# Gathering the experts of 64 tokens, running the other 192 through full products, and starting a transformer kernel in quarters

## The chip, the core and the metric

The kernel runs on one core of a Trainium2 chip. The core has five engines with instruction streams of their own: TensorE (PE in the profile, with its weight loads as PEld), VectorE (DVE), ScalarE (ACT), GpSimd (POOL) and SyncE (SP, which here only issues DMAs). All data comes from HBM through 16 DMA engines. The metric is the device time of one execution in microseconds (us); lower is better.

## The reference, cut to what matters

A two-layer transformer block over 256 tokens with 256 context tokens, then a second block with a convolution and recurrence mixer and a layer of experts (PEER), then a last normalization. The two places that the change touches:

```python
m_lat = silu(c) @ ada_w[i] + ada_b[i]          # 6 x 1024 modulation values; the same with c_ctx
sh1, sc1, g1, sh2, sc2, g2 = split(m_lat, 6)
h  = rms(x, norm1_g[i]) * (1.0 + sc1) + sh1    # hc likewise for the context
f, q, k, v = split(h @ w_in)                   # first projections
...
def peer(x, wq, keys, u_tab, v_tab):           # 256 tokens, 16384 experts
    q = (x @ wq).reshape(B, L, 8, 2, 128)      # 8 heads
    s = einsum('blhpd,hpkd->blhpk', q, keys)
    ts, ti = top_k(s, 16)
    cs, ci = top_k(all pairs of the two halves, 16)
    experts = e1 * 128 + e2                    # 8 * 16 = 128 experts for each token
    act = gelu(einsum('td,tkd->tk', x, u_tab[experts])) * softmax(cs)
    return einsum('tk,tkd->td', act, v_tab[experts])
```

`u_tab` and `v_tab` have 16384 rows of 1024 float32 numbers each (67 MB each).

## The kernel before

**Products.** A float32 product runs as three products in the type fp32r: each operand is split into a high part (a copy by ACT) and a low part (a subtraction by DVE; `split`, L326 and L327), and `mm3` (L331 to L333) multiplies high by high, low by high and high by low into one accumulator in PSUM. A matmul has a stationary operand, loaded as weights (128x128 at most), and a moving one that streams past it, one column after the other; its tile is printed as 128*128 with the moving shape behind it.

**The slab stream.** All weights come as slabs of 128x1024 float32 (512 KB). `Stream.get` keeps loads two slabs ahead: SP issues the DMA into `raw`, ACT makes `hi`, DVE makes `lo`, and a slab of a projection then takes 24 matmuls (8 pieces of the contraction, three products). `crit` is an instruction behind which slab loads are held.

**The start.** Silu of the two conditions is spread over all partitions (`cbc`). The modulations of layer 0 and 1 come from tiles of 128x1024 of the modulation weights, most of them in an idle moment of DVE: one multiply and reduce over 1024 columns (L450) for each of two conditions. The first five tiles (NAK) go to PE instead: `ada_first` (L436) has 128 weight columns stationary and two moving columns. The first 16 tiles must be there before the first norm is applied: 5 by PE, 11 by DVE (22 instructions). Meanwhile `x_sums`, `sums_add` and `sums_done` square x and the context (ACT), add up (POOL, L475), and take the inverse root (POOL, L366). `norm_mod` applies norm and modulation to all 8 pieces of 128 channels, and only then do the slabs of the first projections start, in the order key, value, four queries.

**PEER.** 16 slabs of `peer_wq` and the scores; then a dense computation. All 16384 experts are computed for all 256 tokens, and those that a token did not choose get the gate 0.
- `inner(j, tn)`: slab j of u, stationary, against the 256 tokens as moving columns; gelu into `big[:, j, :]` (128 slabs x 256 tokens). The first J1 = 56 slabs run before and under `select` (the two top-k, on DVE), which lays out expert numbers and gates in `eT`.
- The gates stage: `gates4` takes four tokens at a time. DVE and ACT build one-hot tables (B L1353, A L1363), PE multiplies them (L1365) into the gates of all 16384 experts, DVE multiplies `big` by them. 64 such groups alternate with the other 72 slabs of u.
- The v stage: for each of 128 slabs of v, `big[:, j, :]` is split (`ah`, `al`), and the tokens are stationary (two halves of 128), the slab moving in two halves of 512 columns: 12 matmuls. The four accumulators are [tokens, channels].
- The tail: residual and last norm on DVE and ACT (L1500 the last multiply), four output DMAs.

Tiles are scheduled by a list scheduler at compile time; each engine runs its instructions in order.

## Time and profile before

| what | us |
|---|---|
| median of 3 runs | 2120.29 |
| range of the runs | 2119.91 to 2121.41 |
| the profiled execution | 2122.77 |
| its span, from the first to the last instruction | 2120.9 |

The profiled execution is one execution of the program under the hardware profiler. Its span is 1.9 us shorter than its own time. In a window's row each engine's busy time stands with its number of instructions; a busy PE may still be pausing inside its matmuls, because they are pipelined. [...]

### The profile page before, as it was taken

What the parts mean: (1) busy time and instruction counts of PE and PEld (TensorE: products, weight loads), DVE (VectorE), ACT (ScalarE), POOL (GpSimd) and SP (SyncE); (2) the same over time, 40 slices, a digit from 0 to 9 for tenths busy, and PEclk for the clock granted to TensorE, in tenths of its full rate; (3) what the DMA queues carried; (4) which work ended last, traced back from release to release, by engine and by line L of the source; (5) the groups of instructions that cost most, each with busy time, mean ns of one, the idle gap of its engine ahead of it and who ended that gap; (6) DMA issues with size and microseconds to landing.
All of it is one profiled execution on the core that took longest, in us unless ns stands there. A gap on an engine that the chain in (4) does not pass through costs nothing.

```text
span 2120.9 us, 34014 instructions
## 1 busy us (share of the span) xinstructions
PE 2054.7 (97%) x12714; PEld 1803.1 (85%) x12714; DVE 1511.1 (71%) x2853; ACT 1086.4 (51%) x1997; POOL 150.4 (7%) x194
## 2 busy tenths in 40 slices
PE   6999899999999999999999999999999999999998
PEld 4857677888878857999898999999999998888886
DVE  7795999674756485555578877996677886666666
ACT  3366332332335464444586844555677765454544
POOL 4001100000010001000124311000000000000000
PEclk9989899999999999999999999999999999999999
DMA  8242457796843324555776465556544446566563
GB/s 319 92 140 75 150 195 252 233 328 207 284 136 109 120 87 142 180 186 179 238 255 215 133 195 175 175 189 190 167 146 145 149 149 203 195 192 196 192 195 129
DMA packets 115649, 383.90 MB, mean 181 GB/s; under 512 B 12611, under 2 KB 21092, under 8 KB 115228
## 3 DMA queue, kind: packets, MB, share of 16 engines
q1 hardware_dynamic: 106146, 358.32, 51.6%
q0 software_dynamic: 4048, 15.47, 2.0%
q10 hardware_dynamic: 5290, 7.94, 1.2%
q8 instruction: 100, 1.64, 0.3%
q14 instruction: 65, 0.53, 0.1%
HBM read 366.08 MB, written 15.60 MB: 180 GB/s over the span
## 4 chain that ended last, share of the span: by engine, by line
PE 87%; DVE 5%; ACT 3%; issue 2%; POOL 1%; DMA 1%; SPq 0%; ACTq 0%; DVEq 0%; POOLq 0%
PE pa L331 26%; PE pa L333 25%; PE pa L332 25%; PE pb L1365 3%; PE pb L620 2%; DVE adaj L450 1%; PE pb L607 1%; PE pa L707 1%; DVE lo L327 1%; PE pb L984 1%; PE pa L866 1%; ACT hi L326 1%; DMA adaw<-in_ada_n 1%; POOL ix L1058 0%; PE pb L505 0%
## 5 line engine op out<-in xcount | busy, mean ns | idle before, releaser
L326 ACT ACTIVATE hi<-raw 128x1024 fp32r<-128x1024 f32 (+2 forms) x534 | 552.4, 1037 | 628.9 <-PE pa L332 430.1
L327 DVE TENSOR_TENSOR lo<-raw,hi 128x1024 fp32r<-128x1024 f32 (+2 forms) x534 | 641.6, 1204 | 281.8 <-ACT hi L326 233.4
L331 PE MATMUL pa<-nhi,hi 128*128 128x256 f32 (+1 forms) x1504 | 430.8, 287 | 5.1 <-ACT sg L1214 3.1
L333 PE MATMUL pa<-nhi,lo 128*128 128x256 f32 (+1 forms) x1504 | 425.8, 284 | 0.0
L332 PE MATMUL pa<-nlo,hi 128*128 128x256 f32 (+1 forms) x1504 | 425.7, 284 | 0.0
L331 PEld LDWEIGHTS pa<-nhi,hi 128*128 128x128 f32 x1504 | 286.0, 191 | 6.8 <-ACT sg L1214 3.5
L332 PEld LDWEIGHTS pa<-nlo,hi 128*128 128x128 f32 x1504 | 285.8, 190 | 0.0
L333 PEld LDWEIGHTS pa<-nhi,lo 128*128 128x128 f32 x1504 | 285.6, 190 | 0.0
L332 PE MATMUL pa<-lo,hi 128*128 128x512 f32 (+1 forms) x704 | 238.3, 339 | 0.0
L331 PE MATMUL pa<-hi,hi 128*128 128x512 f32 (+1 forms) x704 | 235.5, 340 | 2.8 <-ACT hi L326 2.7
L333 PE MATMUL pa<-hi,lo 128*128 128x512 f32 (+1 forms) x704 | 236.7, 339 | 0.0
L332 PE MATMUL pa<-lo,ah 128*128 128x512 f32 x512 | 198.9, 389 | 0.0
L333 PE MATMUL pa<-hi,al 128*128 128x512 f32 x512 | 198.2, 389 | 0.0
L450 DVE CUSTOM_DVE_ANT_0 adaj<-adaw,cbc,vec 128x1024 bf16<-128x1024 f32 x150 | 195.7, 1339 | 2.6 <-ACT cbc L420 1.3
L331 PEld LDWEIGHTS pa<-hi,hi 128*128 128x128 f32 x704 | 134.8, 193 | 19.0 <-ACT hi L326 3.3
L332 PEld LDWEIGHTS pa<-lo,hi 128*128 128x128 f32 x704 | 135.3, 192 | 14.7 <-DVE lo L520 0.8
L333 PEld LDWEIGHTS pa<-hi,lo 128*128 128x128 f32 x704 | 135.2, 192 | 13.8
L326 ACT ACTIVATE ah<-big 128x256 fp32r<-128x256 f32 x128 | 53.4, 418 | 168.5 <-PE pa L332 167.1
L331 PE MATMUL pa<-hi,ah 128*128 128x512 f32 x512 | 138.9, 389 | 0.0
L331 PE MATMUL pa<-fh,hi 128*128 128x512 f32 (+1 forms) x352 | 117.7, 337 | 0.5 <-ACT hi L326 0.5
L332 PE MATMUL pa<-fl,hi 128*128 128x512 f32 (+1 forms) x352 | 117.8, 336 | 0.0
L333 PE MATMUL pa<-fh,lo 128*128 128x512 f32 (+1 forms) x352 | 116.5, 336 | 0.0
(376 smaller groups left out, 3540.8 us busy)
## 6 DMA issues: line engine op xcount, KB each, us to landing
raw<-in_u SPq DMA_DIRECT2D x128, 512.0 KB, 3.5
raw<-in_v SPq DMA_DIRECT2D x128, 512.0 KB, 4.3
adaw<-in_ada_n SPq DMA_DIRECT2D x91, 512.0 KB, 4.4
raw<-in_ffn_gu SPq DMA_DIRECT2D x88, 512.0 KB, 3.5
raw<-in_w_in SPq DMA_DIRECT2D x63, 512.0 KB, 4.5
raw<-in_ffn_d SPq DMA_DIRECT2D x32, 512.0 KB, 3.5
raw<-in_od_in SPq DMA_DIRECT2D x24, 512.0 KB, 3.5
low<-lo POOLq DMA_DIRECT2D x19, 512.0 KB, 5.5
```

The source lines that it names most:

```text
L326: self.nc.scalar.activation(out=hi, in_=src, func=AF.Copy)
L327: return self.nc.vector.tensor_tensor(lo, src, hi.bitcast(F32), op=ALU.subtract)
L331: mm(ps, L[0], R[0], start=start, stop=False)
L332: mm(ps, L[0], R[1], start=False, stop=False)
L333: self.last_mm = mm(ps, L[1], R[0], start=False, stop=stop)
L450: nc.vector.tensor_tensor_reduce(j, w, self.cbc[:, s, :], 1.0, self.v(f"ada_b{l}", m), ALU.mult, ALU.add, accum_out=self.mods[l][:, m, s:s ...
L607: nc.tensor.transpose(pt[:, k, :], P[:, e, 128 * k:128 * k + 128], self.ident)
L620: self.nc.tensor.matmul(po[b, :], vt(e, k), PTs[e][:, k, :], start=k == 0, stop=k == kc - 1)
L707: nc.tensor.matmul(S[kv], qT[i][b, q0:q0 + 128], kT[b, k0:k0 + nk], start=True, stop=True)
L866: nc.tensor.matmul(S[e], qT[b, i, 128 * qt:128 * qt + 128], kT[b, i, :], start=True, stop=True)
L984: nc.tensor.matmul(ps, raw[:tn, c, tc, :], kp[c][:tn, tc, :], start=tc == 0, stop=tc == 2)
L1365: nc.tensor.matmul(ps[:, k, :], A, B[:, k, :], start=True, stop=True)
```

## The change

**The start.** NAK is 16. `ada_block(b)` computes four modulation tiles on PE with the condition stationary (32 columns, of which two are used, in one of four column strips) and 512 weight columns moving, 8 matmuls in float32; a copy by ACT and four small matmuls add the strips and turn the result. Block b gives shift and scale of channels 256 b to 256 b + 255. DVE's 22 reductions and `ada_first` go. `cbc` is made by 16 matmuls and four DVE copies. `first_sums` adds squares on DVE instead of POOL and takes the inverse root on DVE. Four slab loads are issued between block 0 and block 1; `first_products` applies norm and modulation to two channel pieces as each block is done, and multiplies them with the first four slabs (key, value, two queries).

**PEER.** The last 64 tokens (TS) no longer go through the dense computation. `sparse` takes 64 steps over u and 64 over v. On the 128 partitions stand the 64 tokens twice. Step c issues an indirect DMA from POOL that gathers one row of u into each partition (512 KB): of each token's 128 experts, number c into its first and number 64 + c into its second partition. DVE multiplies them with x and reduces (128x1024); gelu and gate follow once for all. A step over v gathers likewise, and DVE multiplies and adds (128x1024) into `acc`, whose two halves are added at the end by a matmul for each 512 channels. Five buffers (NROW) take the gathered rows. Of the 129 steps 46 stand in the gates stage, one in each group from the third on, and 83 under the first 112 slabs of v. The dense part has 192 tokens (TD): the u products have 192 moving columns, there are 48 groups of gates with 1.5 slabs each, and the v products are turned round: 24 matmuls a slab with v stationary and 192 tokens moving, into accumulators [channels, tokens], which are zeroed by four matmuls at first and transposed back in the tail by 16.

```diff
-NAK = 5
+NAK = 16
...
 J1, J2 = 56, 128
+TS = 64
+TD = 256 - TS
+NROW = 5
...
+        self.cz = ap.tile([128, 8, 32], F32, name="cz")
+        nc.gpsimd.memset(self.cz, 0.0)
+        nc.scalar.activation(out=self.cz[:, :, 0:2], in_=self.vv("c").rearrange("p (k s) -> p k s", s=2), func=AF.Silu)
+        self.strips = ap.tile([128, 2], F32, name="strips")
+        nc.vector.tensor_reduce(self.strips, self.ident.rearrange("p (j c) -> p c j", j=4)[:, 0:2, :], AX.X, ALU.add)
...
+    def ada_block(self, b):
+
+
+        nc = self.nc
+        ps = self.pb()
+        for q in range(4):
+            w = self.ada_load(self.a["ada_p"][4 * b + q])
+            for i in range(2):
+                k = 2 * q + i
+                j = 32 * (k % 4)
+                nc.tensor.matmul(ps[j:j + 32, :], self.cz[:, k, :], w[:, 512 * i:512 * i + 512], start=k < 4, stop=k >= 4)
+        r = self.awp.tile([128, 512], F32, tag="adar", name="adar", bufs=2)
+        nc.scalar.copy(r, ps)
+        pt = self.pb([128, 4, 2])
+        for i in range(4):
...
+        bias = bias[:, :, 2 * b:2 * b + 2].unsqueeze(3).to_broadcast([128, 2, 2, 2])
+        mods = self.mods[0][:, 0:16, :].rearrange("p (h k) s -> p h k s", h=2)[:, :, 2 * b:2 * b + 2, :]
+        nc.vector.tensor_tensor(mods, pt.rearrange("p (h k) s -> p h k s", h=2), bias, op=ALU.add)
+        g = self.vv("n1_0")[:, 2 * b:2 * b + 2].unsqueeze(2)
+        nc.vector.scalar_tensor_tensor(self.gsc[0][:, 0, 2 * b:2 * b + 2, :], self.mods[0][:, 8 + 2 * b:10 + 2 * b, :], 1.0,
+                                       g.to_broadcast([128, 2, 2]), op0=ALU.add, op1=ALU.mult)
...
+    def first_sums(self):
+
+        nc, pool = self.nc, self.np
+        ps = self.pb([128, 4])
+        for s, src in enumerate((self.xb[:, :, X0:X0 + T], self.cb)):
+            acc = pool.tile([128, 2, T], F32, tag="sq", name="sqa", bufs=2)
+            for k in range(0, KC, 2):
+                t = acc if k == 0 else self.awp.tile([128, 2, T], F32, tag="sqf", name="sqf", bufs=2)
+                nc.scalar.activation(out=t, in_=src[:, k:k + 2, :], func=AF.Square)
+                if k:
+                    nc.vector.tensor_tensor(acc, acc, t, op=ALU.add)
...
+        out = [self.pb()[:, :T] for _ in range(2)]
+        for s in range(2):
+            for i in range(2):
+                nc.tensor.matmul(out[s][:, 128 * i:128 * i + 128], y[:, 2 * s + i:2 * s + i + 1].to_broadcast([128, 128]),
+                                 self.ident, start=True, stop=True)
...
+    def first_products(self, p):
+
+        nc, st = self.nc, self.st
+        hi = p.tile([128, KC, 512], F32R, tag="hhi", name="nh")
+        lo = p.tile([128, KC, 512], F32R, tag="hlo", name="nl")
+        self.ada_rows()
+        self.ada_block(0)
+        bc = self.first_sums()
+        self.xw, self.nxw = self.awp, (2, 1, 0)
+        for _ in range(4):
+            st._load()
+        for b in range(1, 4):
...
+        self.crit = self.ld.ins
+        for _ in range(4):
+            st._split()
...
+        first = [(self.pa(),) + st.out.pop(j)[:2] for j in range(4)]
+        st.i = 4
+        for b in range(4):
+            ks = [2 * b, 2 * b + 1]
+            for k in ks:
...
+                    self.norm_apply(self.x_part(s), T, bc[s], self.np, lambda k: hi[:, k, c], lambda k: lo[:, k, c],
+                                    lambda k: self.gsc[0][:, 0, k, s:s + 1], lambda k: self.mods[0][:, k, s:s + 1], [k])
...
+            for ps, wh, wl in first:
+                for k in ks:
+                    w = slice(128 * k, 128 * k + 128)
+                    self.mm3(ps, (wh[:, w], wl[:, w]), (hi[:, k, :], lo[:, k, :]), k == 0, k == KC - 1)
+        return hi, lo, [f[0] for f in first]
...
-        self.awp, self.nada = self.open("a0"), 7
+        self.awp, self.nada = self.open("a0"), 12
...
-            if j == 0:
-                nc.sync.dma_start(out=self.xb, in_=xin[:, :, :TB])
...
+        nc.sync.dma_start(out=self.xb, in_=xin[:, :, :TB])
+        nc.sync.dma_start(out=self.cb, in_=xin[:, :, TB:])
+        hi, lo, first = self.first_products(p)
...
+        if tt:
+            f = [t.rearrange("p a b -> p (a b)") for t in (e[0], e[1], go)]
+            nc.vector.scalar_tensor_tensor(sp["eg"][:, 0, :], f[1], 128.0, f[0], op0=ALU.mult, op1=ALU.add)
+            nc.vector.tensor_copy(sp["eg"][:, 1, :], f[2])
+            ps = self.pb([128, 2, 128])
+            nc.tensor.matmul(ps.rearrange("p a b -> p (a b)"), sp["sel"], sp["eg"].rearrange("p a b -> p (a b)"),
+                             start=True, stop=True)
+            for h in range(2):
+                w = slice(64 * h, 64 * h + 64)
+                nc.vector.tensor_copy(sp["ix"][w, :], ps[w, 0, w])
+                nc.vector.tensor_copy(sp["g"][w, :], ps[w, 1, w])
...
+        xt = x.tile([128, KC, 2, TS], F32, name="xt")
         self.spg = self.token_rows(self.open("ht", side="right"))
-        self.norm_apply(self.x_part(0), T, self.sums_done(fill=self.fill)[0], self.np,
+        bc = self.sums_done(fill=self.fill)[0]
+        self.norm_apply(self.x_part(0), T, bc, self.np,
                         lambda k: hi[:, k, :], lambda k: lo[:, k, :], lambda k: self.v("g_ffn", k))
+        for k in range(KC):
+            for h in range(2):
+                nc.vector.scalar_tensor_tensor(xt[:, k, h, :], self.xb[:, k, X0 + TD:X0 + T], self.v("g_ffn", k),
+                                               bc[:, TD:], op0=ALU.mult, op1=ALU.mult)
...
         def inner(j, tn):
 
-            ps = self.pa()[:, :T]
-            self.proj(ps, self.st.get(), rhs)
+            ps = self.pa()[:, :TD]
...
         for j in range(J1):
             inner(j, 0)
-        for tt in range(2):
-            self.select(tm, s, tt, num, eT)
+        for tt in (1, 0):
+            self.select(tm, s, tt, num, eT, sp)
+        rows = self.sparse(p, sp)
         jc = J1
-        for t0 in range(0, T, 4):
+        for t0 in range(0, TD, 4):
             self.gates4(g, t0, iota, eT, big, jc)
-            while jc < 128 and (jc - J1) * T < (J2 - J1) * (t0 + 4):
+            while jc < 128 and (jc - J1) * TD < (J2 - J1) * (t0 + 4):
                 inner(jc, t0 + 4)
                 jc += 1
+            if t0 >= 8:
+                next(rows)
         for j in range(jc, 128):
-            inner(j, T)
...
-        acc = [self.pa() for _ in range(4)]
-        hq = [g.tile([128, D], F32, name=f"hq{tt}") for tt in range(2)]
+        z = g.tile([128, 2 * TD], F32R, name="z")
+        nc.vector.memset(z.bitcast(F32), 0.0)
+        acc = [self.pa([128, 2, TD]) for _ in range(4)]
+        for t in acc:
+            nc.tensor.matmul(t.rearrange("p a b -> p (a b)"), z[:, :128], z, start=True, stop=False)
...
+        def dense(j, k, ah, al, wh, wl):
+            w = slice(128 * k, 128 * k + 128)
+            o = acc[k // 2][:, k % 2, :]
+            for l, r in ((wh, ah), (wh, al), (wl, ah)):
+                self.last_mm = nc.tensor.matmul(o, l[:, w], r, start=False, stop=j == 127 and k % 2 == 1 and l is wl)
...
+        left = 2 * TS + 1 - (TD // 4 - 2)
         for j in range(128):
-            ah = p.tile([128, T], F32R, tag="ah", name="ah", bufs=3)
...
+            held.append((ah, al) + self.st.get())
             if j < 128 - HELD or j == 127:
...
+                for k in range(KC):
+                    for n, h in enumerate(held):
+                        dense(j + 1 - len(held) + n, k, *h)
+                    if j == 127 and k % 2:
+                        (nc.vector.tensor_copy if k % 4 == 3 else nc.scalar.copy)(yt[:, k - 1:k + 1, :], acc[k // 2])
                 held = []
-            if j == 100:
+            for _ in range((j + 1) * left // 112 - j * left // 112 if j < 112 else 0):
+                next(rows)
...
+            if j == 112:
+                for c in range(2):
+                    r = slice(512 * c, 512 * c + 512)
+                    ps = self.pb()
+                    nc.tensor.matmul(ps[64:128, :], sp["fold"], sp["acc"][:, r], start=True, stop=True)
+                    nc.vector.tensor_tensor(hq[1][64:128, r], hq[1][64:128, r], ps[64:128, :], op=ALU.add)
...
+                pt = self.pb([128, 4, 128])
+                for k in range(4):
+                    nc.tensor.transpose(pt[:n, k, :], yt[:, 4 * c + k, 128 * tt:128 * tt + n], self.ident)
+                nc.vector.tensor_tensor(hv[:n], hv[:n], pt[:n].rearrange("p a b -> p (a b)"), op=ALU.add)
...
+    def sparse(self, p, sp):
+
+        nc, a = self.nc, self.a
+
+        def row(name, c):
+            r = p.tile([128, D], F32, tag="row", name="row", bufs=NROW)
+            nc.gpsimd.indirect_dma_start(out=r, out_offset=None, in_=a[name].rearrange("j p d -> (j p) d"),
+                                         in_offset=bass.IndirectOffsetOnAxis(ap=sp["ix"][:, c:c + 1], axis=0))
+            return r
+
+        for c in range(TS):
+            r = row("ur", c)
+            d = p.tile([128, D], BF16, tag="sd", name="sd", bufs=1)
+            nc.vector.tensor_tensor_reduce(d, r, sp["x"], 1.0, 0.0, ALU.mult, ALU.add, accum_out=sp["h"][:, c:c + 1])
+            yield
+        nc.scalar.activation(out=sp["a"], in_=sp["h"], func=AF.Gelu_apprx_tanh)
+        nc.vector.tensor_tensor(sp["a"], sp["a"], sp["g"], op=ALU.mult)
+        nc.gpsimd.memset(sp["acc"], 0.0)
+        yield
+        for c in range(TS):
+            r = row("v", c)
+            nc.vector.scalar_tensor_tensor(sp["acc"], r, sp["a"][:, c:c + 1], sp["acc"], op0=ALU.mult, op1=ALU.add)
+            yield
```

## Rows read from the trace of the kernel before

**Rows 1.** The page's first line and its busy times by engine.

```profile
span 2120.9 us, 34014 instructions
...
PE 2054.7 (97%) x12714; PEld 1803.1 (85%) x12714; DVE 1511.1 (71%) x2853; ACT 1086.4 (51%) x1997; POOL 150.4 (7%) x194
```

**Rows 2.** Windows (us, five engines busy, PEclk, DMA share, GB/s): start and PEER stages.

```profile
0.00:51.10 51.10, 30.18 (x112) 24.98 (x112) 39.64 (x73) 17.75 (x34) 24.13 (x25) 1.00 0.87 316
...
1350.00:1507.00 157.00, 157.00 (x1346) 157.00 (x1345) 124.45 (x348) 83.09 (x129) 0.00 (x0) 1.00 0.57 186
1507.00:1764.00 257.00, 256.98 (x2217) 256.60 (x2216) 204.56 (x393) 183.52 (x526) 0.00 (x0) 1.00 0.45 148
1764.00:2111.40 347.40, 347.36 (x1533) 287.28 (x1531) 211.30 (x265) 173.94 (x259) 0.00 (x0) 1.00 0.59 190
2111.40:2120.90 9.50, 0.00 (x0) 0.00 (x0) 5.46 (x17) 0.72 (x2) 0.00 (x0) 0.66 0.29 110
```

**Rows 3.** Windows of the densest transfers, same columns.

```profile
10.00:20.00 10.00, 5.45 (x25) 5.08 (x24) 8.16 (x13) 3.42 (x9) 4.49 (x3) 1.00 1.05 392
424.00:477.00 53.00, 53.00 (x235) 43.89 (x234) 41.06 (x55) 20.52 (x25) 2.69 (x5) 1.00 0.92 328
```

**Rows 4.** Timeline of the start (start us, us, instruction): DVE, PE, ACT.

```profile
24.25 2.27 DVE L450 CUSTOM_DVE_ANT_0 adaj<-adaw,cbc,vec 128x1024 bf16<-128x1024 f32 x1
...
31.07 1.27 DVE L450 CUSTOM_DVE_ANT_0 adaj<-adaw,cbc,vec 128x1024 bf16<-128x1024 f32 x1
...
51.14 1.65 PE L331 MATMUL pa<-nh,hi 128*128 128x512 f32 x3 [1.11 <-ACT nh L519]
...
77.30 0.58 ACT L647 ACTIVATE sq<-pa 128x512 f32<-128x512 f32 x1
```

**Rows 5.** Timeline of PE in the PEER up-projections, 256 moving columns.

```profile
1603.02 0.28 PE L331 MATMUL pa<-nhi,hi 128*128 128x256 f32 x1
...
1605.47 0.28 PE L331 MATMUL pa<-nhi,hi 128*128 128x256 f32 x1
```

**Rows 6.** Timeline of PE in the PEER value products, 512 moving columns.

```profile
2086.72 1.07 PE L331 MATMUL pa<-hi,ah 128*128 128x512 f32 x4
...
2089.44 0.84 PE L331 MATMUL pa<-hi,ah 128*128 128x512 f32 x3
```

**Rows 7.** Timeline of PE at 623 us, one moving column each.

```profile
623.70 0.36 PE L493 MATMUL pb<-ones,sq 128*128 128x1 f32 x2
...
625.04 0.36 PE L493 MATMUL pb<-ones,sq 128*128 128x1 f32 x2
```

**Rows 8.** Weight loads by tile or line (ns min/median/max, start us, forms).

```profile
L331 PEld LDWEIGHTS pa<-hi,ah x512: 186/188/188, 1762.9 to 2110.3; 128*128 128x128 f32 x171
...
L332 PEld LDWEIGHTS pb<-vl,df x18: 152/157/158, 1103.7 to 1159.2; 128*91 128x91 f32 x12, 16*91 16x91 f32 x6
...
L493 PEld LDWEIGHTS pb<-ones,sqa x38: 92/192/338, 27.7 to 1286.8; 128*128 128x128 f32 x36, 128*16 128x16 f32 x2
```

**Rows 9.** VectorE and ACT groups by form (busy us, mean ns, idle before).

```profile
L327 DVE TENSOR_TENSOR lo<-raw,hi 128x1024 fp32r<-128x1024 f32 x502 | 615.0, 1228 | 271.4 <-ACT hi L326 229.3 <-DMA low<-lo 27.9 <-PE pa L333 5.9
...
L327 DVE TENSOR_TENSOR al<-big,ah 128x256 fp32r<-128x256 f32 x128 | 54.4, 425 | 69.4 <-ACT ah L326 69.4
...
L1500 DVE SCALAR_TENSOR_TENSOR o<-hq,fy,gf x4: 746/750/752, 2112.4 to 2116.5; 128x512 f32<-128x512 f32 x4
```

**Rows 10.** Waits in the gates stage (us in total, times, longest).

```profile
DVE A L1363 <- PE pb L1365: 40.3, 109, 0.8
```

**Rows 11.** GpSimd's cheapest DMA issue and dearest instruction (ns min/median/max).

```profile
L294 POOL DMA_DIRECT2D low<-lo x24: 533/533/578, 339.7 to 591.8; - x24
...
L1084 POOL TENSOR_TENSOR ix<-r,ix x4: 2520/2579/2860, 1100.2 to 1221.4; 128x1088 f32<-128x1088 f32 x4
```

**Rows 12.** PE's f32 products of 256 columns, in two column halves.

```profile
758.38 1.95 PE L620 MATMUL pb<-PT,vt 128*64 128x256 f32 x16
```

**Rows 13.** The page's DMA issues of the slabs (KB each, us to landing).

```profile
raw<-in_v SPq DMA_DIRECT2D x128, 512.0 KB, 4.3
```

More of the change, by code (lines that the diff above doesn't have):

```diff
@@ L525, in x_part @@
         return lambda k: self.cb[:, k, :]
+    def first_sums(self):
[9 more added lines that the diff above has]
+            for i in range(2):
+                for j in range(2):
+                    nc.tensor.matmul(ps[:, 2 * s + i:2 * s + i + 1], acc[:, j, 128 * i:128 * i + 128], self.ones[:, 0:1],
+                                     start=j == 0, stop=j == 1)
+        v = pool.tile([128, 4], F32, tag="nv", name="nv", bufs=1)
+        nc.vector.tensor_scalar(v, ps, 1.0 / D, EPS, op0=ALU.mult, op1=ALU.add)
+        y = self.rsqrt(v, 4, pool, "n4")
+        out = [self.pb()[:, :T] for _ in range(2)]
+        for s in range(2):
+            for i in range(2):
+                nc.tensor.matmul(out[s][:, 128 * i:128 * i + 128], y[:, 2 * s + i:2 * s + i + 1].to_broadcast([128, 128]),
+                                 self.ident, start=True, stop=True)
+        return out
@@ L621, in pair_values, with l0 @@
         return po
-    def l0(self, p, hi, lo):
+    def l0(self, p, hi, lo, first):
         nc, a = self.nc, self.a
@@ L657, in l0 @@
         kT = at.tile([128, 512], F32, name="kT")
-        ps = self.pa()
-        self.proj(ps, self.st.get(), rhs)
+        ps = first[0]
         ssk = self.pb([128, 4, 2])
@@ L670, in l0 @@
         rope_x(kT)
-        ps = self.pa()
-        self.proj(ps, self.st.get(), rhs)
+        ps = first[1]
         vf = at.tile([128, 512], F32, tag="P", name="vf", bufs=self.npb)
@@ L683, in l0 @@
         for i in range(4):
-            ps = self.pa()
-            self.proj(ps, self.st.get(), rhs)
+            ps = self.pa() if i > 1 else first[2 + i]
+            if i > 1:
+                self.proj(ps, self.st.get(), rhs)
             ssq = self.pb([128, 4, 2])
@@ new lines, in peer @@
+        nc.vector.memset(z.bitcast(F32), 0.0)
+        acc = [self.pa([128, 2, TD]) for _ in range(4)]
+        for t in acc:
+            nc.tensor.matmul(t.rearrange("p a b -> p (a b)"), z[:, :128], z, start=True, stop=False)
+        hq = [g.tile([128, D], F32, name=f"hq{n}") for n in range(2)]
+        gf = g.tile([128, D], F32, name="gf")
+        yt = g.tile([128, KC, TD], F32, name="yt")
+        def dense(j, k, ah, al, wh, wl):
[3 more added lines that the diff above has]
+                self.last_mm = nc.tensor.matmul(o, l[:, w], r, start=False, stop=j == 127 and k % 2 == 1 and l is wl)
@@ L1467, in peer @@
             if j < 128 - HELD or j == 127:
-                for tt in range(2):
-                    wait = self.tc.issue_after(self.last_mm.ins) if tt and j == 127 else contextlib.nullcontext()
-                    with wait:
-                        for c in range(2):
-                            for h in held:
-                                rows(tt, c, *h)
+                for k in range(KC):
[3 more added lines that the diff above has]
+                        (nc.vector.tensor_copy if k % 4 == 3 else nc.scalar.copy)(yt[:, k - 1:k + 1, :], acc[k // 2])
@@ L1576, in build @@
         self.softplus4()
-        self.l0(p, hi, lo)
+        self.l0(p, hi, lo, first)
         self.l1()
```

116 lines of the change are left out of this document (57 added, 59 removed).

## The prediction

> **What bounds the kernel now.** I read the busy times first: PE is busy for 97% of a span of 2120.9 us [rows 1]. That says where to look, not what a change is worth, since a busy PE may be waiting for its weights. So I read the windows by stage next [rows 2]. In the three dense parts of PEER (56 u slabs 157 us, gates 257 us, v slabs 347.4 us) PE is busy all the time while DVE has 20% or more to spare; at the start PE is busy 30 of 51 us, the DMA engines 87%. So the start is bound by bytes and by what follows them, PEER by the pace of matmuls. The timelines give that pace. With 256 moving columns 21 matmuls take 2.45 us, 116.7 ns each [rows 5]; with 512 columns 12 take 2.72 us, 226.7 ns each [rows 6]. The two lie on a line of 0.43 ns a column. What a narrower matmul takes, no fp32r row shows; with one column 12 float32 matmuls at the same clock take 1.34 us, 111.7 ns each [rows 7]. So the moving columns stop paying somewhere below 256. The weight loads say why: an fp32r load of 128 columns is recorded with 188 ns, one of 91 columns with 157, a float32 load of 128 with 192, one of 16 with 92 [rows 8]. That is 0.84 to 0.89 ns a column, 107 to 114 ns for 128, whatever moves; and there are as many loads as matmuls [rows 1].
>
> **The start.** Before, the first projection starts at 51.14 us and the fourth is done at 77.30 [rows 4]. DVE's reductions take 2.27 us beside POOL's additions and 1.27 without [rows 4]; 22 of them, 28 to 50 us, leave DVE's path. After, 16 tiles of 0.524 MB, x and the context (2.2 MB) and four slabs (2.1 MB) must land: 12.7 MB, at the 316 GB/s of this stretch [rows 2] 40 us, at the densest 392 [rows 3] 32. I take 39. Behind the last block come eight float32 products of which two wait for the last tile (0.9), ACT's copy (0.6), four small products (0.9), two small DVE steps (0.4), norm and split of the first pieces (3.4 with their handshakes) and a last quarter of 24 products at 0.227 [rows 6], 5.4: some 12 us. The first three quarters run under the arriving tiles. Four projections are then done at 51 to 55 us, against 77.3: I take -22. [...] ACT's and DVE's moved additions (L475 on POOL before) run under the transfers; without that cover they cost 6 instructions of some 0.7 us. SP issues the four slabs behind block 0, so that 2.1 MB come ahead of twelve tiles; the sum of bytes has that.
>
> **The u products, 192 columns instead of 256.** The first 56 slabs are 1344 matmuls. By columns each takes 116.7 - 64 x 0.43 = 89 to 93 ns, by the load 111.7. I take 111.7, because one-column products can be held up by nothing but their loads, and the load's slope gives the same number from other rows: 1344 x 5 ns = -7. Bounds -31 and 0.
>
> [...]
>
> **The gates stage.** PE now: 72 x 24 x 0.1117 = 193 for u, and the groups' own products, before (257 - 72 x 24 x 0.1167) / 64 = 0.87 each [rows 2, 5], 42 for 48 groups: 235. DVE: before 204.56 / 64 = 3.2 us a group [rows 2]. A group now carries 1.5 slabs for 1.125 (0.375 x about 1.4, the low part of 1.23 [rows 9] and a product) and, in 46, a row reduction of 1.27 [rows 4]: 48 x 3.73 + 46 x 1.27 = 238. Both engines are near full and feed each other in order: DVE waited 109 times, 40.3 us, for the gates' products [rows 10], waits that were slack and now cost. I take 252, -5; bounds -19 (238) and +15 (a third of the waits stays on top). Each reduction waits for a gather. Behind it on DVE stand `lo` of the next slab and B and A of the next group, for which PE waits. Five buffers let POOL run five gathers ahead, some 25 us, against a landing of 4.3 us for SP's like [rows 13]; that covers it.
>
> **The v stage.** Twice as many matmuls, each narrower: 3072 x 0.1117 = 343 for 1536 x 0.2267 = 348: -5. By columns 3072 x 0.0934 = 287. DVE in one of the first 112 slabs: `lo` 1.23, `al` at 192 columns 0.36 (0.425 less 64 x 1.05 ns, the slope between its two forms [rows 9]) and 0.74 gather steps. One is twice the 512 columns of the 0.75 us form with one overhead: 1.29 [rows 9]. Sum 2.54 for PE's 2.68: it holds, with 5% to spare. Bytes: 0.524 x 1.74 = 0.91 MB in 2.68 us, 340 GB/s, where the kernel has moved 328 to 392 at best [rows 3]. For that crowding, which also delays SP's slabs, +4; bounds 0 and +25.
>
> **The rest.** The tail gets four copies, 16 transposes and additions behind them: +4 (2 to 6) on 9.5 us [rows 2]. Sixteen small multiplications for `xt`, eight transposes, the index work and four zeroing products come in front of PEER's stages or between them, where nothing on their engines is surely free: +3 (0 to 5).
>
> Sum: 2122.8 - 22 - 7 - 5 - 5 + 4 + 4 + 3 = 2095 for the profiled execution, which lies 2.5 above the median of the runs: **2093**. Its own range is 2075 to 2117, from the bounds of start, gates and crowding.
>
> **Rivals.**
>
> *The columns decide.* If the floor of rows 7 belongs to float32 alone, 192 columns take 93 ns: u -31; gates limited by DVE, 238 and some coupling, -12; v limited by DVE (112 x 2.54 + 16 x 2.24 = 320) or by bytes at 392 GB/s, about 312, -36. 2122.8 - 22 - 31 - 12 - 36 + 7, less 2.5: 2026. For it: the two fp32r forms lie on a line. Against: equal load times of both types. Chance 0.13.
>
> [...]
>
> *Slower: GpSimd makes the gathers too slowly.* No run of before has an indirect DMA. The nearest rows are a plain issue, 0.53 us, and POOL's dearest instruction, 2.6 us [rows 11]; both leave it idle most of the time. In the v stage 83 steps share 302 us, 3.6 us each. With a pace g the stage lasts 83 g + 43. It eats all else that is gained from g = 4.0; at 5 us it lasts 458, and the total is 2203. Chance 0.08.
>
> [...]
>
> *Slower: each gather step holds DVE.* If a step costs 0.4 us more, by a late landing, a longer instruction, or a handshake, DVE needs 2.84 in a v slab (+13 over before) and the gates stage +11: 2122, no gain. At 0.7 us it is 2163. For it: DVE has 5% to spare and runs in order. Against: POOL runs ahead. Chance 0.12.
>
> *Slower by far: fewer than 256 columns at float32's rate.* Every fp32r product of before has 256 columns or more. Float32's 256 columns take up to 1.95 / 8 = 0.24 us for a pair of column halves [rows 12], 0.95 ns a column: 183 ns for 192, and 6144 x 71 ns = 438 more: 2530. Chance 0.07.
>
> **How the numbers follow.** The main line holds 0.60. Faster: 0.57 of it, and the columns' 0.13: 0.70. The same, within 0.2% (2116 to 2124.5), about what a measurement of this kernel can tell: 0.05, from the ends of the main line and the held DVE. Slower: the rest of these and the two far rivals, 0.25. The range must reach both the columns' case and the held DVE at 0.7 us: 2024 to 2163; the two far rivals, 0.15, lie outside.
>
> **What would show it.** Matmuls of 192 columns 111 to 112 ns apart (93: the columns decide; 180: float32's rate). The fourth projection done near 53 us. The gates stage near 252 us with DVE busy 95%; the v stage 343 to 350 us, DMA share over 0.9 and POOL mostly idle. If POOL is busy throughout the v stage, or DVE waits for a row's DMA at every step, a slower rival has it. The prediction goes wrong most easily at the pace of the 192-column matmuls, on which both PEER terms hang.

## The result, and the profile after

The changed kernel takes 2130.68 us in the median of 6 runs (2130.26 to 2139.41), the kernel before 2120.83: a ratio of 1.0059, with a 95% interval of 1.0038 to 1.0080. It is slower by 0.6%, where 2093 was forecast; the range of 2024 to 2163 held it, the sign did not. The profiled execution took 2130.43 us, 1.7 more than its span.

The page of the changed kernel, its first line, its busy times, and the gathers' issues among the costliest groups:

```profile
span 2128.7 us, 37168 instructions
...
PE 2032.2 (95%) x14196; PEld 1831.0 (86%) x14196; DVE 1582.1 (74%) x2991; ACT 1062.8 (50%) x1913; POOL 318.9 (15%) x308
...
L1649 POOL DMA_INDIRECT row<-in_ur,six x64 | 91.9, 1436 | 317.7 <-DVE sg L1429 197.0
```

PE has less to do than before (2032.2 for 2054.7 [rows 1]) in a longer span. Windows of the changed kernel (the third number from the end of a row is TensorE's granted clock as a share of its full speed, before the DMA share and GB/s): the start up to the first projection and up to the end of the first four; the u slabs before the gates in two parts; gates; v in two parts; tail.

```profile
0.00:31.00 31.00, 19.16 (x97) 12.14 (x97) 18.32 (x53) 15.63 (x24) 0.94 (x7) 0.84 0.96 361
31.00:59.80 28.80, 28.80 (x156) 21.68 (x152) 12.29 (x32) 7.83 (x16) 0.00 (x0) 1.00 0.48 187
1327.20:1480.00 152.80, 152.80 (x1369) 152.70 (x1368) 120.39 (x353) 80.33 (x123) 0.34 (x1) 1.00 0.65 196
1480.00:1505.60 25.60, 16.14 (x139) 15.39 (x137) 22.76 (x40) 8.77 (x16) 16.53 (x12) 0.94 0.91 338
1505.60:1748.60 243.00, 227.26 (x1972) 225.09 (x1973) 240.43 (x457) 164.44 (x443) 95.13 (x66) 0.97 0.85 291
1748.60:1900.00 151.40, 141.17 (x1136) 137.27 (x1136) 132.77 (x148) 60.90 (x93) 85.11 (x51) 0.93 0.93 343
1900.00:2116.70 216.70, 216.70 (x1943) 216.70 (x1942) 118.59 (x159) 104.40 (x160) 0.00 (x0) 1.00 0.62 186
2116.70:2128.70 12.00, 2.05 (x19) 1.78 (x18) 8.28 (x29) 2.57 (x8) 0.00 (x0) 0.79 0.23 87
```

Compare with [rows 2]. Before, PE is busy throughout the three parts of PEER. Now each part has a hole. Between 1480 and 1505.6 it works 16.1 of 25.6 us; there DVE and the DMA engines are nearly full. In the gates stage it works 227.3 of 243.0. And between 1748.6 and 1900 it works 141.2 of 151.4; there the transfers stand at 343 GB/s and 0.93 of the DMA engines' time. From 1900 on, POOL is idle: every gather is done, and PE is full again.

Idle time is not the whole loss. The granted clock averages 0.94, 0.97 and 0.93 in these three stretches, and 1.00 in the two beside them where PE never waits. No window of 5 us in this profile has less than 0.50, and windows of 2 us in the v stage show 0.50 from 1814 to 1818 and from 1854 to 1860 us. If all of the missing share was lost at 0.50, PE ran at it for some 39 us in all (an estimate: twice the missing share of each stretch), 21 of them in the v stage. One 20 us window of that stage shows what this does: in 18.48 busy us PE does 134 matmuls, 138 ns each, where the stretch from 1900 on has 1943 in 216.7 us, 111.5 ns each.

```profile
1804.00:1824.00 20.00, 18.48 (x134) 18.14 (x134) 16.64 (x19) 6.92 (x11) 11.99 (x8) 0.83 1.01 396
```

Stage by stage, from the first matmul of each stage to that of the next, in the profiled executions of both kernels and of the experiments below. The wq slabs come before the u slabs; tail is what follows the start of the last v product. In brackets stand the u slabs that PE did before the first gate product.

| us | up to wq | wq | u before gates (slabs) | gates | u + gates | v | tail | span |
|---|---|---|---|---|---|---|---|---|
| before | 1291.8 | 53.1 | 158.7 (56) | 259.3 | 418.0 | 348.1 | 9.9 | 2120.9 |
| after | 1270.8 | 56.3 | 178.4 (62) | 243.0 | 421.4 | 368.1 | 11.9 | 2128.7 |
| e1 start only | 1274.8 | 53.0 | 158.7 (56) | 259.3 | 418.0 | 348.1 | 9.3 | 2103.2 |
| e2 index first | 1275.5 | 55.4 | 177.2 (57) | 253.6 | 430.8 | 349.9 | 11.9 | 2123.5 |
| e3 spread in v | 1273.8 | 55.4 | 177.7 (62) | 236.5 | 414.2 | 347.2 | 11.9 | 2102.4 |
| e4 = e2 + e3 | 1278.6 | 55.4 | 178.5 (57) | 239.9 | 418.4 | 347.0 | 11.9 | 2111.3 |
| e5 spread in gates too | 1277.9 | 55.5 | 168.1 (62) | 231.0 | 399.1 | 346.5 | 11.9 | 2090.8 |
| e6 = e5 + index first | 1275.2 | 55.4 | 152.0 (56) | 242.4 | 394.4 | 346.9 | 11.9 | 2083.8 |
| e7 five gathers only | 1275.0 | 55.5 | 178.1 (62) | 246.1 | 424.2 | 347.4 | 11.9 | 2113.9 |
| e8 no rows on DVE | 1281.7 | 55.6 | 170.5 (62) | 231.0 | 401.5 | 359.3 | 11.9 | 2110.0 |
| e9 ten rows earlier | 1275.9 | 55.4 | 130.8 (48) | 263.8 | 394.6 | 347.2 | 11.9 | 2084.9 |
| e10 128 columns | 1273.7 | 55.4 | 152.1 (56) | 242.4 | 394.6 | 621.8 | 12.0 | 2357.4 |
| e11 one product at the start | 1266.8 | 55.6 | 152.0 (56) | 242.4 | 394.4 | 346.9 | 11.9 | 2075.6 |

The first column varies by 11 us among kernels whose code is the same there (the kernel before, e1 and e11 apart), so single stages are the better measure. The difference of the spans is 7.8 us: -21.0 up to wq, +3.2 wq, +19.7 u, -16.3 gates, +20.0 v, +2.0 tail, each rounded.

The slabs in brackets matter. A u slab is 24 matmuls, 2.7 us at the pace below, so the six slabs that the changed kernel does early are 16 of the 19.7 us by which its u is longer, and the same 16 us are what its gates stage seems to save. Where the brackets differ, u + gates is the measure: 3.4 us longer than before, where 12 less was forecast.

How the hole before the gates comes about can be read on two engines. PE's timeline of the changed kernel: two u products 36 matmuls apart, then the product that turns the top-k's expert numbers into gather indices.

```profile
1473.77 0.28 PE L335 MATMUL pa<-nhi,hi 128*128 128x192 f32 x1
...
1477.79 0.28 PE L335 MATMUL pa<-nhi,hi 128*128 128x192 f32 x1
...
1478.12 0.62 PE L1424 MATMUL pb<-big 128*128 128x256 f32 x2
```

VectorE's timeline there (start, duration, instruction, idle before and its releaser):

```profile
1420.42 0.29 DVE L1417 TENSOR_TENSOR big<-big 128x256 bf16<-128x256 bf16 x1
...
1478.78 0.22 DVE L1428 CAST six<-pb 64x64 uint32<-64x64 f32 x1 [0.93 <-PE pb L1424]
...
1484.69 1.23 DVE L1656 CUSTOM_DVE_ANT_0 sd<-row,sx 128x1024 bf16<-128x1024 f32 x1 [1.71 <-DMA row<-in_ur,six]
...
1485.84 1.22 DVE L1415 TENSOR_TENSOR big<-big 128x2048 bf16<-128x2048 bf16 x1
...
1502.08 0.68 DVE L1436 COPY eT<-pb 128x128 f32<-128x128 f32 x3
...
1504.02 1.29 DVE L1446 TENSOR_TENSOR B<-iota,eT 128x512 f32<-128x512 f32 x2
```

After 1420.42 DVE does nothing for 58 us but split slabs, one of 1.23 us every 2.68, though the second top-k (128 tokens) isn't finished: by the code, its last steps write tiles that the transposes of the first have yet to read, and those stand behind the index product in PE's queue, which is behind the first 56 slabs of u and runs at 1478.12. Only then do the gathers begin, and row reductions (`sd<-row`, L1656) come between the top-k's steps, of which the first waits 1.71 us for its gather with a step of the top-k behind it (L1415). The expert numbers are there at 1502.08 (`eT`), the gate tables start at 1504.02. The waits from 1327 to 1506 us (engine, releaser, us in total, times, longest) show POOL's side:

```profile
POOL row L1649 <- DVE sg L1429: 197.0, 1, 197.0
```

### The profile page after: what moved, and what is told of

Read it like the earlier page. It is cut to its first block, busy times and chain, and to the rows that moved or that the text cites. A ratio compares the mean times of both kernels' runs of the same rounds, so it can differ in the third digit from the quotient of the medians.

```text
span 2128.7 us, 37168 instructions
## 1 busy us (share of the span) xinstructions
PE 2032.2 (95%) x14196; PEld 1831.0 (86%) x14196; DVE 1582.1 (74%) x2991; ACT 1062.8 (50%) x1913; POOL 318.9 (15%) x308
## 4 chain that ended last, share of the span: by engine, by line
PE 81%; DVE 8%; issue 4%; DMA 3%; ACT 3%; POOL 1%; SPq 0%; ACTq 0%; DVEq 0%; POOLq 0%
PE pa L335 20%; PE pa L336 19%; PE pa L337 19%; PE pa L1586 13%; DVE lo L331 2%; PE pb L1458 2%; DVE adaj L475 2%; PE pb L702 1%; ACT hi L330 1%; DMA row<-in_v,six 1%; PE pb L689 1%; PE pb L1065 1%; PE pa L947 1%; DVE P L671 1%; DVE sacc L1664 1%
## 5 line engine op out<-in xcount | busy, mean ns | idle before, releaser
L335 PE MATMUL pa<-nhi,hi 128*128 128x192 f32 (+2 forms) x1504 | 420.7, 281 | 10.0 <-ACT big L1551 5.0
L337 PE MATMUL pa<-nhi,lo 128*128 128x192 f32 (+2 forms) x1504 | 418.9, 279 | 1.8 <-DVE lo L331 1.8
L336 PE MATMUL pa<-nlo,hi 128*128 128x192 f32 (+2 forms) x1504 | 420.0, 280 | 0.0
L1586 PE MATMUL pa<-ah,hi 128*128 128x192 f32 x1024 | 276.8, 279 | 7.0 <-ACT hi L330 7.0
L1586 PE MATMUL pa<-al,hi 128*128 128x192 f32 x1024 | 278.6, 278 | 1.9 <-DVE al L331 1.9
L1586 PE MATMUL pa<-ah,lo 128*128 128x192 f32 x1024 | 266.7, 279 | 1.4 <-DVE lo L331 0.9
L1586 PEld LDWEIGHTS pa<-ah,hi 128*128 128x128 f32 x1024 | 199.2, 196 | 8.7 <-ACT hi L330 8.7
L1586 PEld LDWEIGHTS pa<-al,hi 128*128 128x128 f32 x1024 | 200.8, 196 | 2.2 <-DVE al L331 2.2
L1586 PEld LDWEIGHTS pa<-ah,lo 128*128 128x128 f32 x1024 | 191.8, 196 | 2.6 <-DVE lo L331 2.5
L1649 POOL DMA_INDIRECT row<-in_ur,six x64 | 91.9, 1436 | 317.7 <-DVE sg L1429 197.0
```

The costliest lines, as they stand in the source:

```text
L335: mm(ps, L[0], R[0], start=start, stop=False)
L336: mm(ps, L[0], R[1], start=False, stop=False)
L337: self.last_mm = mm(ps, L[1], R[0], start=False, stop=stop)
L1586: self.last_mm = nc.tensor.matmul(o, l[:, w], r, start=False, stop=j == 127 and k % 2 == 1 and l is wl)
L1649: nc.gpsimd.indirect_dma_start(out=r, out_offset=None, in_=a[name].rearrange("j p d -> (j p) d"), in_offset=bass.IndirectOffsetOnAxis(ap=s ...
```

## The experiments

What each of them leaves out is said with it; the others compute all. All are compared with the kernel before on the same chip. e7, e8, e10 and e11 ran once each, the others four times or more; the stages are those of one profiled execution of each.

**e1: the start alone.** The changed kernel with the methods `select` and `peer` of before:

```diff
-        for tt in (1, 0):
-            self.select(tm, s, tt, num, eT, sp)
-        rows = self.sparse(p, sp)
+        for tt in range(2):
+            self.select(tm, s, tt, num, eT)
...
```

> The change's start with the experts of before. Theory A (the start gives its 21 us for good, the experts' part costs 29): 2097 to 2102. Rival (the 21 us at the start are given back behind it, since the same modulations are needed later): 2110 or more.

2103.49 us (ratio 0.9916, 0.9900 to 0.9933): -18. The start's gain stays, a little smaller than theory A had it; so the experts' part costs 27 us.

**e2: the index product first.** In `select`, the index product, the transposes and the copies behind them get a priority of 5000 ahead in the list scheduler:

```diff
+        self.tc.cur_priority -= 5000
         if tt:
             f = [t.rearrange("p a b -> p (a b)") for t in (e[0], e[1], go)]
...
         nc.vector.tensor_scalar(eT[3][:, w], pt[:, 0, :n], -1.0, None, op0=ALU.mult)
+        self.tc.cur_priority += 5000
```

> The changed kernel, with the index product and the transposes of the top-k planned ahead of the u slabs on TensorE. Theory A (the second top-k and the gathers stand behind an index product that TensorE runs only at 1478 us): the u stage falls from 178 to 150 to 156 us, the gathers start near 1400 us, the total is 2095 to 2110. Rival B (VectorE simply has too much to do, so that a step done sooner in one stage is missing in the next): u stage shorter, gates or v longer by the same, total 2124 to 2135.

2125.28 us (1.0018, 1.0008 to 1.0027). Theory A fell: the gathers did start before 1400, but the u stage took 177.2 us, with five slabs fewer in it, and u + gates grew from 421.4 to 430.8. The scheduler let the row reductions follow their gathers at once, 45 of them before 1508 us, between the steps of the second top-k. Two windows of e2 from 1400 on:

```profile
1400.00:1420.00 20.00, 17.77 (x153) 17.08 (x152) 20.00 (x53) 7.90 (x12) 9.62 (x8) 1.00 1.01 387
1420.00:1440.00 20.00, 16.68 (x139) 16.00 (x139) 20.00 (x52) 8.36 (x13) 10.24 (x8) 0.98 0.94 352
```

DVE is full, the transfers are at 352 to 387 GB/s, and PE works 17.8 and 16.7 of 20 us. Only v is shorter (349.9), because most rows are done before it: the crowd has moved into another stage. The total lies in rival B's range, but B had the u stage shorter and a later one longer; it went the other way. Theory A' came out of this: the rows' instructions must be kept apart, not only brought forward.

**e3: the rows spread over v.** Each row step of the v stage is ordered behind the split `al` of its slab on VectorE. The gathers then follow as buffers come free:

```diff
-            self.split(ah, al, big[:, j, :])
+            sp_al = self.split(ah, al, big[:, j, :])
...
-                next(rows)
+                with self.tc.issue_after(sp_al.ins):
+                    next(rows)
```

> The changed kernel, with VectorE's row steps of the v stage held behind the split of their slab, 0.89 steps a slab over 112 slabs, instead of most of them in the first 45. Theory A (crowding: transfers at 360 to 370 GB/s with DVE at 90% make TensorE wait): v stage 348 to 354 instead of 368 us, total 2110 to 2117. Rival B (the work of DVE in the v stage has to be paid wherever it lies): v stage 365 or more, total 2125 or more.

2103.34 us (0.9914, 0.9898 to 0.9931), v 347.2: theory A for the v stage. The total is 7 us below its lower end, as much as the gates stage is shorter (236.5 for 243.0), into which the steps of the v stage can no longer run ahead.

**e4: e2 and e3 together**, the two edits shown.

> e2 and e3 together. Theory A: both gains add up, 2080 to 2095. Rival B: 2120 or more.

2107.48 us (0.9934, 0.9918 to 0.9951; the profiled execution took 2113.03): between the two theories, and not added up. v is right at 347.0, but u + gates is 418.4, 4 us more than in e3. As in e2 the rows, let loose early, fill the u stage.

**e5: the rows spread over the gates too.** On top of e3:

```diff
-            self.gates4(g, t0, iota, eT, big, jc)
+            grp = self.gates4(g, t0, iota, eT, big, jc)    # returns the instruction that makes B
...
             if t0 >= 8:
-                next(rows)
+                with self.tc.issue_after(grp.ins):
+                    next(rows)
```

> e3, and each row step of the gates stage is held behind the one-hot table of its group, so that none runs between the steps of the second top-k. Theory A' (the row steps pulled forward, seven of them in the u stage with full transfers beside them, delay the second top-k, whose rest already stands behind the index product): u stage 160 to 168 us for 178, gates stage 238 to 245, total 2088 to 2097. Rival B (what is taken from the u stage comes back in the gates stage, where DVE is the limit): gates 250 or more, total 2100 to 2106.

2092.15 us (0.9860, 0.9844 to 0.9877). u 168.1, at the upper edge, and the gates 231.0, better than both theories had it: together 399.1 for 414.2, with the same slabs in each. What left the u stage did not come back. The hole in it is closed:

```profile
1333.30:1501.40 168.10, 168.10 (x1507) 168.00 (x1505) 133.96 (x377) 87.90 (x138) 7.05 (x5) 1.00 0.67 207
```

**e6: e5 with the edit of e2.**

> e5 with the index product and the transposes ahead of the u slabs. Theory A' (the late index product costs the rest, and e2 hid that by letting 44 gathers into the u stage): u stage 150 to 154 us, gates 238 to 245, v 347, total 2074 to 2086. Rival (the u stage is set by DVE's top-k in any order): u stage 165 or more, no better than e5.

2086.06 us (0.9835, 0.9818 to 0.9851), 35 us under before, 45 under the changed kernel. The u stage falls to 152.0, but mostly because the six slabs go back into the gates: PE had no hole in e5's u stage that could be closed. u + gates falls from 399.1 to 394.4, and these 5 us are what the early index product is worth once the rows are held back. Windows of e6: u up to 1480, gates, the first 151 us of v:

```profile
1330.60:1480.00 149.40, 149.40 (x1339) 149.30 (x1338) 125.92 (x370) 79.55 (x126) 5.59 (x5) 1.00 0.67 212
...
1482.60:1725.00 242.40, 237.39 (x2118) 237.25 (x2117) 228.80 (x433) 162.12 (x454) 79.32 (x47) 0.99 0.76 264
1725.00:1876.00 151.00, 151.00 (x1337) 151.00 (x1336) 126.87 (x165) 72.25 (x111) 68.61 (x41) 0.99 0.92 329
```

PE is full in u and in the first part of v, with DMA at 0.92 there, where the changed kernel had 0.93; but it has 41 gathers in this part and the changed kernel 51, 329 GB/s for 343. So the mean DMA share does not tell a crowd: windows of 20 us reach 402 GB/s in the changed kernel and 344 in e6. The 5.0 us that PE is idle in the gates are one wait, for the zeros that DVE writes for the accumulators of v (`z`):

```profile
PE pa L1581 <- DVE z L1578: 5.0, 1, 5.0
```

The changed kernel waits 6.4 us there, the kernel before not at all. An earlier zeroing was not tried.

**e7: the gathers away, DVE's steps kept.** Only the first five gathers are issued, the later steps read these five buffers again (the experts of the last 64 tokens are left out):

```diff
+            if len(held) == NROW:
+                held.append(held.pop(0))
+                return held[-1]
-            r = p.tile([128, D], F32, tag="row", name="row", bufs=NROW)
+            r = p.tile([128, D], F32, name=f"row{len(held)}")
+            held.append(r)
```

> The changed kernel with only the first five of 128 gathers: all later row steps read these five buffers again (the experts of the last 64 tokens are left out). VectorE's work and its order stay nearly the same. If transfers are what the bunched steps crowd: v stage 347 to 352 us for 368, u stage unchanged. If VectorE is: v stage 362 or more.

v 347.4, u 178.1, total 2115.66 us: in the v stage it is the transfers. Here is the same stretch of v in e7:

```profile
1754.70:1906.00 151.30, 151.30 (x1321) 149.81 (x1320) 145.62 (x163) 70.92 (x108) 0.00 (x0) 0.98 0.63 189
```

DVE is even fuller (145.6 of 151.3 us), and PE has no hole. In u and gates it is not the transfers: without them u + gates takes 424.2 us for 421.4, with the same slabs in each, and PE has the same holes.

**e8: the gathers kept, DVE's steps away.** The row steps work on 16 columns for 1024 (the experts of the last 64 tokens are left out):

```diff
-nc.vector.scalar_tensor_tensor(sp["acc"], r, sp["a"][:, c:c + 1], sp["acc"], ...)
+nc.vector.scalar_tensor_tensor(sp["acc"][:, :16], r[:, :16], sp["a"][:, c:c + 1], sp["acc"][:, :16], ...)
```

and likewise the reduction over u.

> The changed kernel with all 128 gathers, but VectorE's row steps cut from 1024 to 16 columns (the experts of the last 64 tokens are left out). If transfers are what crowds: v stage 360 or more, since the gathers now come even faster. If VectorE is: 347 to 352.

v 359.3, total 2111.75 us. 0.7 under the number that was set for transfers, but 12 over the stage without crowding, with DVE half idle (54.2 us of the first 100). The gathers, no longer held by DVE, run further ahead, so that fewer are left for the v stage. The issues in its first 151 us, in the changed kernel and in e8:

```profile
row<-in_v,six POOLq DMA_INDIRECT x51
...
row<-in_v,six POOLq DMA_INDIRECT x30
```

30 gathers cost 12 us, and 51 cost the changed kernel 21: 0.4 us for each in both, where e6's 41, spread out, cost nothing. So e8 shows no part of DVE's in the v stage. In u and gates it is the other way round: u + gates falls from 421.4 to 401.5. The gates stages of e7 (no gathers) and of e8 (no row work on DVE):

```profile
1508.50:1754.60 246.10, 231.60 (x1973) 229.18 (x1973) 240.63 (x457) 164.26 (x443) 0.00 (x0) 0.95 0.47 145
...
1507.80:1738.80 231.00, 224.19 (x1973) 222.80 (x1974) 182.26 (x482) 161.25 (x445) 97.11 (x89) 0.99 0.97 359
```

With 145 GB/s and DVE nearly full (98%) PE is idle for 14.5 us; with 359 GB/s and DVE at 79% it is idle for 6.8. So early row steps cost the v stage by their transfers, and the u and gates stages by their time on DVE.

**e9: ten row steps before the gates.** e6, with ten steps between the second top-k and the first group (36 left in the gates):

```diff
+        for _ in range(10):
+            with self.tc.issue_after(end.ins):     # the last instruction of select
+                ur = next(rows)
...
+            with self.tc.issue_after(ur.ins):
+                grp = self.gates4(g, t0, iota, eT, big, jc)
```

> e6 with ten of the gates stage's 46 row steps put between the second top-k and the first group of gates, one for each u slab. If the gates stage is limited by VectorE (238 us of work in 242): gates 228 to 236, u stage 152 to 156, total 2076 to 2083. Rival (gathers at one a slab crowd the u slabs, as they did in e2): u stage 160 or more, no gain over e6's 2086.

2085.72 us (0.9827, 0.9810 to 0.9843): no gain, and no crowd either. u and gates together take 394.6 us, as in e6 (the border between them moved: only 48 slabs are done before the first gate product). So in e6 it is no longer DVE's row work that sets the gates stage. PE's own work in both stages is 128 x 24 x 0.1117 + 48 x 0.87 = 385 us of 394, and 5.0 of the rest are the wait for `z`.

**e10: 128 moving columns.** e6, with 128 for 192 columns in the v products (the experts' values of tokens 128 to 191 are left out):

```diff
-            o = acc[k // 2][:, k % 2, :]
-            for l, r in ((wh, ah), (wh, al), (wl, ah)):
+            o = acc[k // 2][:, k % 2, :128]
+            for l, r in ((wh, ah[:, :128]), (wh, al[:, :128]), (wl, ah[:, :128])):
```

> e6 with 128 moving columns for 192 in the v products (the experts' values of tokens 128 to 191 are left out). If the weight load sets the pace: spacing 110 to 113 ns as with 192 columns, v stage 345 to 349 us. If the columns still counted (0.42 ns each): spacing 67 to 85 ns, v stage 300 to 320, where VectorE is the limit.

Neither number for the stage: v took 621.8 us and the total 2359.21. The windows of v show why, and the timeline of PE at its beginning and near its end:

```profile
1727.50:2310.00 582.50, 582.50 (x2741) 580.06 (x2740) 265.82 (x326) 149.55 (x229) 70.64 (x75) 0.50 0.57 171
2318.00:2345.00 27.00, 27.00 (x244) 27.00 (x244) 13.30 (x19) 11.41 (x18) 0.00 (x0) 1.00 0.34 109
```

```profile
1722.27 1.62 PE L1581 MATMUL pa<-z 128*128 128x384 f32 x4 [5.01 <-DVE z L1578]
...
2302.27 3.14 PE L1617 MATMUL pb<-sacc,fold 128*64 128x512 f32 x4
...
2329.85 0.28 PE L1590 MATMUL pa<-ah,hi 128*128 128x128 f32 x1
...
2331.19 0.28 PE L1590 MATMUL pa<-ah,hi 128*128 128x128 f32 x1
```

For 582 us the granted clock was 0.50, though PE was busy without a pause: 2741 matmuls in 582.5 us, 213 ns each. It fell at the 5.0 us wait for `z` (0.52 in the mean from 1718 to 1800 us), which e6 has too and after which the grant was 0.90 in the first 20 us of its v stage and 1.00 in the next 20. Here it came back only when four products of 512 columns ran (`fold`, 2302 us), and the 128-column products behind them kept it. What brings it back, these runs do not separate. At a grant of 1.00, 12 matmuls take 1.34 us, 111.7 ns each, the spacing of 192 columns and of one column [rows 7]. So at 192 columns, 128 and one the moving columns do not set the pace; what does takes 111.7 ns at a grant of 1.00 and 213 at 0.50. That it is the load of the stationary operand rests on the slope of rows 8; no run changed the number of stationary columns.

**e11: a third of the start's products.** e6, with the product of the high parts alone in the first four projections (their two small products are left out):

```diff
-                    self.mm3(ps, (wh[:, w], wl[:, w]), (hi[:, k, :], lo[:, k, :]), k == 0, k == KC - 1)
+                    nc.tensor.matmul(ps, wh[:, w], hi[:, k, :], start=k == 0, stop=k == KC - 1)
```

> e6 with only the product of the high parts in the four first projections, 32 matmuls for 96 (their two small products are left out). If the start is bound by TensorE from the first norm on: the last of these products starts near 46 to 49 us for 59.8, 64 x 0.227 = 14.5 us sooner at most. If it is bound by the tiles' bytes and the norm's chain: 54 us or later.

2077.44 us; the first and the last group of these 32 products in PE's timeline:

```profile
31.07 2.22 PE L606 MATMUL pa<-nh,hi 128*128 128x512 f32 x8
...
46.50 1.19 PE L606 MATMUL pa<-nh,hi 128*128 128x512 f32 x4 [0.36 <-ACT nh L544]
```

They are done at 47.7 us, 12 sooner than the 96, of 14.5 at most. TensorE sets the start from the first norm on.

## Why the prediction was wrong

**The step that failed: where the row steps run.** The sum charged one row step to each gates group ("in 46, a row reduction") and 0.74 to each v slab, as the loop writes them. The list scheduler runs them as soon as they are ready: seven over u started before the first gate product, six of them among the last steps of the second top-k, the other 57 over u and 11 over v in the gates stage, and the remaining 53 over v in the first 140 us of the v stage (to 1888). Their first and last starts on DVE, over u and over v:

```profile
L1656 DVE CUSTOM_DVE_ANT_0 sd<-row,sx x64: 1209/1217/1226, 1484.7 to 1709.6; 128x1024 bf16<-128x1024 f32 x64
...
L1664 DVE SCALAR_TENSOR_TENSOR sacc<-row,sa,sacc x64: 1161/1279/1290, 1716.4 to 1887.0; 128x1024 f32<-128x1024 f32 x64
```

Held where the loop writes them, and with nothing else changed, the kernel takes 2092.15 us (e5), where 2093 was forecast. That it comes so close is partly luck: in e5's profile the part up to wq is 14 us shorter for the 22 taken, and u + gates 19 shorter for the 12 taken. Misplaced, the steps cost 38 us (2130.68 to 2092.15).

**The pace of the matmuls was right.** 36 matmuls of 192 columns take 4.02 us in the u stage: 111.7 ns, the value taken. e10 shows that fewer moving columns do not change it; that the load is the reason, as the prediction had it, fits but was not tested by itself. The rivals of the columns (93 ns) and of float32's rate (183) are out.

**The u products and the gates.** The u term was "-7", from the matmuls alone, with 0 to -31 as bounds, and the pace delivered it: with 56 slabs and no wait the stage has 152.0 us (e6), 6.7 under before. What the sum lacked is who releases the gates: the second top-k on DVE. Row steps between its steps cost 9.6 us of u, and those in the gates 5.5 of that stage (e3 to e5, the same slabs in each). In front of it stands a new product on PE between two halves of DVE work. I had put the index work under "the rest", +3 with its other parts, as work, not as a wait, and did not ask what stands ahead of it in PE's queue. That late place costs 5 us of u + gates (e5 to e6), as PE runs six slabs of the gates ahead meanwhile.

**The v stage: a size, within its bound.** "-5" for the products came out as -1.2: 346.9 in e6 for 348.1, though the pace was the one taken. Of the other 4 some 2 are the lower clock behind the wait for `z` (4 us of it, an estimate from the grant of 0.90). The crowding's "+4; bounds 0 and +25" was the right mechanism at the wrong size: 368.1 is 21 over e6. I had spread 83 steps evenly, 0.74 a slab at 340 GB/s. The stage got 53, one every 2.6 us, a slab's time. Spread over 112 slabs as I had assumed, the transfers cost nothing (e3: 347.2), and bunched the 21 us vanish without the transfers (e7). About half of the 21 is PE's idle time, 10.2 us. Most of the rest is the lower clock: some 21 us at e10's 213 ns a product instead of 111.7 lose 10 (an estimate). The sum has no term for it.

**The start.** "I take -22": -18 (e1). The bytes were faster than assumed, 407 to 409 GB/s at 10 to 31 us in the windows of the changed kernel, and the last of them was there by 45 us. What failed is "the first three quarters run under the arriving tiles". The first norm was ready at 31 us, and from then PE was busy without a pause to 59.8 (28.8 of 28.8 us): all four quarters of the products, and two of the four blocks, were still to do. e11 confirms it. The forecast's range also rests on bounds for the start, the upper one with PE at half its pace over its products; no run shows that: in the changed kernel the grant was 0.99 from 31 to 45 us and 1.00 from there to 59.8.

```profile
10.00:20.00 10.00, 8.24 (x50) 4.44 (x48) 7.41 (x15) 5.83 (x9) 0.00 (x0) 1.00 1.03 409
20.00:31.00 11.00, 5.92 (x29) 2.67 (x28) 8.39 (x22) 3.64 (x6) 0.00 (x0) 0.54 1.03 407
...
45.00:60.00 15.00, 15.00 (x72) 12.08 (x68) 7.06 (x18) 4.23 (x9) 0.04 (x1) 1.00 0.12 36
```

**Gates, tail and the rest.** Gates: -5 taken. The -16.3 measured is the six slabs that had gone ahead. e6, with 72 slabs in the stage and the row steps held to their groups, has -16.9, so the 14 us for two full engines in order were not needed there. Tail and extras: +4 and +3 forecast, +2.0 and +3.2 measured; the wait for `z`, 5.0 to 6.4 us, was in neither.

**The rivals.** GpSimd's gathers were no limit: an issue takes 1.44 us in the mean over u and 1.64 over v, inside the bounds of 0.53 and 2.6, though the longest takes 3.4. "Each gather step holds DVE" had the right size (2122 to 2163). Its place was u and gates, where the row steps came in front of the work that releases PE (e8 against e7). In the v stage, where it was priced as well, it is out. The waits of the changed kernel's v stage:

```profile
PE pa L1586 <- ACT hi L330: 7.0, 5, 1.4
...
DVE sacc L1664 <- DMA row<-in_v,six: 5.0, 3, 4.5
```

DVE waited three times for a row, 5.0 us in all; PE waited more for the slabs' high parts, the half of a split that DVE has nothing to do with.

What remains of the experts' part, once ordered, is 2086.06 for e1's 2103.49: 17 us. Fewer gate groups save 16 x 0.87 = 14 on PE, and 5 ns at each of 3072 u products 15; the wait for `z` (5), the extras and the tail (5 in all) take most of the difference back. It is not a quarter of the products. Why the scheduler put the index product so late was not tried; the trace shows only where it stands.

## What to carry to other kernels

Work that is given to engines with spare time is done when a scheduler finds it ready, not where the loop writes it: order it explicitly behind the work of its share, or count it at full rate where it first can run. When a new small product feeds a gather or a later stage, look for its place in the queue of the fullest engine before pricing its work. And price a matmul by the larger of a floor, here 111.7 ns (213 where the grant was 0.50), and its columns: from 256 columns down fewer tokens save at most 5 ns of 116.7 here. Look also at the granted clock behind each wait of TensorE: here the lower clock cost about as much in the v stage (some 10 us, an estimate) as the waits themselves (10.2 us).

## What the runs showed of the hardware

In e10 the grant fell to 0.50 at a 5.0 us wait and stayed there for 582 us, though PE was busy without a pause with 128 columns moving behind each load (213 ns a product). It rose near 2304 us (an estimate from its mean of 0.64 from 2200 to 2345), where four products of 512 columns ran (from 2302.27 us), and 128 columns behind them then ran at 1.00 (2318 to 2345 us), 111.7 ns a product. With 192 columns in the same place, behind the same wait (e6), the grant averaged 0.99 over the first 151 us. The v stage of e10, which ran once, took 275 us more than e6's.

Gathers of 512 KB in the first 151 us of the v stage, on top of its slabs, cost 12 us where 30 came bunched (e8), 21 where 51 did, and nothing where 41 were spread (e6), while in the gates stage of e8 359 GB/s in the mean left PE 97% busy.

From 10 to 31 us the changed kernel's core moved 407 to 409 GB/s, where the denser of the two windows of before had 392 [rows 3].
